# Attention scores by pairs of heads: f16 parts on two 64-row tiles, q turned by DMA, scales per token and for all keys

## The chip, the core and the metric

The kernel runs on one core of a Trainium2 chip. The metric is the device time of one execution in microseconds; the median of three runs of the kernel before is 1756.97 us (1756.92 to 1758.68). The profile shown is of one further execution, which took 1763.98 us; its span is 1762.1 us.

The engines are PE (matmul; PEld are its weight loads), DVE (vector), ACT (activation functions, copies with a scale), POOL (a slower vector engine) and SP, whose queue issues DMA transfers. Each engine runs its own instructions in order, and waits on semaphores for those of others.

## The reference

Two layers over 256 tokens of width 2048, with a context of 256 tokens. Layer 0 is a Fourier branch, layer 1 attention with 64 query heads of width 64 and 8 key heads; then a final norm. The part that the change touches, cut:

```python
q = _axial_rope(q.reshape(b, n, ATTN_Q_HEADS, ATTN_HEAD_DIM), rows, cols)
k = _axial_rope(k.reshape(b, n, ATTN_KV_HEADS, ATTN_HEAD_DIM), rows, cols)
...
s = jnp.einsum('bqhgd,bkhd->bhgqk', q, k).astype(jnp.float32) * (ATTN_HEAD_DIM ** -0.5)
s = jnp.where(mask, s, NEG_INF)
p = jax.nn.softmax(jnp.concatenate([s, sk], axis=-1), axis=-1)[..., :-1]
return jnp.einsum('bhgqk,bkhd->bqhgd', p.astype(v.dtype), v)
...
y = jnp.moveaxis(o, 0, 1).reshape(b, n, D_BRANCH) * jax.nn.silu(z)
x = x + gate * (y @ w_out[i])
```

The keys of a query are those of a window and the context, 512 columns in all; `sk` is a learned sink per head. All inputs are float32.

## The kernel before, in words

float32 products are made of parts. An operand is split into a high part (rounded) and a low part (what is left), as fp32r or as f16 with a scale, and a product is three matmuls, high by high, high by low and low by high (`mm3`, lines 145 to 147).

**Layer 1** starts at some 1085 us with the projections of keys and values, and its attention runs from 1132 to some 1610 us. The projections of q and of the gate z, and the first column block of the output product, are cut into *units* (`emit_unit`): 12 matmuls of 512 columns for q, 24 of 256 for z. A unit needs a wh and a wl, the parts of its weights: SP loads 1 MB of raw weights for two units (`raw`, line 50), ACT makes wh (line 66), DVE makes wl (line 67). Two of these tiles per unit and six buffers let the split run at most three units ahead. Units are put between the steps of attention, so that PE has work while the softmax runs on the other engines.

**Attention** is done for the 64 heads one after another. A *group* is the eight heads of one key head, a *block* a pair of heads (b = 0 to 31).

- When the eight units of a group's q are done, `finish_q` copies q out of PSUM (line 1357) and applies the rotary embedding, on POOL except for group 0. `prep_kk` makes the key parts kkh (ACT) and kkl (POOL, line 1346), both halves of the 128 partitions alike.
- `q_turn` turns q on PE with fp32 transposes (line 1370, eight a group), ACT copies the high part (lines 1373, 1374), and DVE subtracts it to get the low part (lines 1375, 1376). High and low part of one head lie above each other in the 128 partitions, so that one matmul with kkh gives two of the three products.
- `stage_s` is S(i), for one head: per 128 tokens two matmuls of fp32r (lines 1483, 1484), a mask and a minimum on DVE (line 1485, the *mask reduction*), then on ACT the exponential p (1488) and the sink's es (1489), on DVE the sum sm and its reciprocal (1490, 1491), then f, the f16 parts of the normalised p (ACT 1500, DVE 1501). A DMA transpose on SP's queue (line 1503) turns each f to ft.
- `stage_o` is P·V, O(b), for a pair of heads: 24 matmuls of 64 output columns (line 1519). The two heads use the two halves of the array's columns, so they come as couples.
- For the last three heads, PE turns f instead (`stage_t`, line 1510).

**The order.** The program is written as: S(i), a unit, after every second head O of the pair before, a unit. A scheduler takes that as a priority and fixes each engine's order ahead of time; on the chip it does not change. PSUM has eight banks of 512 columns. Tiles p and f have three buffers, ft four.

Of the kernel before, what the change touches and what calls it, by code (L numbers as in the profile page):

```python
# [32 lines left out]
def tile_dit(ctx: ExitStack, tc: tile.TileContext, a: dict, out: bass.AP):  # L33
# [10 lines left out]
    def psum():  # L44
        return pp.tile([P, 512], F32, tag="ps", name="ps")
# [1094 lines left out]
    with tc.tile_pool(name="h1", reuse_waits="tile", bufs=16) as h1p:  # L1140
        hx1 = []
        v01, vs = [], []
        dsc = h1p.tile([P, 8], F32, name="dsc", bufs=1)
        kT = []
        with tc.tile_pool(name="kvp", reuse_waits="tile", bufs=2) as kvp:
            hz, ends = [], []
# [75 lines left out]
            for tb in range(4):  # L1222
                t, ab = act(), act(F32R)
                S.copy(t, o[tb][1])
                S.activation(ab, o[tb][1], AF.Abs)
                vs.append((t, ab))
                t = act()
                if tb < 2:
                    roped(t, o[tb][0], tb, actp, "act", tab=ropek)
                else:  # L1230
                    S.activation(t, o[tb][0], AF.Copy, scale=dnk)
                kr.append(t)

            sums2(True)
            V.tensor_reduce(yq[:, 17:18], scn, axis=AX.X, op=ALU.add)
            l1 = psum()
            for tb in range(4):
                PE.matmul(l1, oner, vs[tb][1], start=tb == 0, stop=tb == 3)
            l1s, up_, ex = act(), act(), act(I32)
            V.tensor_scalar(l1s, l1, 2.0**-96, None, op0=ALU.max)  # L1240
            V.tensor_scalar(ex, l1s.bitcast(I32), 23, None, op0=ALU.logical_shift_right)
# [18 lines left out]
        with tc.tile_pool(name="at", reuse_waits="tile", bufs=2) as at:  # L1260
# [61 lines left out]
            ident16 = []  # L1322

            def k_turn(hp):
                o = psum()
                for tb in range(4):
                    PE.transpose(o[:, tb * P : (tb + 1) * P], kr[tb][:, hp * P : (hp + 1) * P], ident)
                t = act()
                S.copy(t, o)
                kT.append(t)  # L1330

            def d_turn(half):
# [3 lines left out]
                V.tensor_scalar(dsc[:, half * 4 : half * 4 + 4], o[:, 0::P], dnk, None, op0=ALU.mult)  # L1336

            def prep_kk(hk):
                kkh = at.tile([P, 512], F32R, tag="kkh", name="kkh")
                kkl = at.tile([P, 512], F32R, tag="kkl", name="kkl")  # L1340
                b = (hk % 2) * 64
                src = kT[hk // 2][b : b + 64, :]
                for c in (0, 64):
                    S.copy(kkh[c : c + 64, :], src)
                for c in (0, 64):
                    GP.tensor_tensor(kkl[c : c + 64, :], src, kkh[b : b + 64, :].bitcast(F32), op=ALU.subtract)
                kk[hk] = (kkh, kkl)

            def finish_q(hk, oq):
                qr = []  # L1350
                for tb in range(2):
                    t = act()
                    if hk == 0:
                        roped(t, oq[tb], tb, actp, "act")
                    else:
                        t0 = act()
                        S.copy(t0, oq[tb])
                        roped(t, t0, tb, actp, "act", GP)
                    qr.append(t)
                if hk:  # L1360
                    prep_kk(hk)
                for p2 in range(2):
                    defer.append((slot[0], lambda p2=p2: q_turn(hk, p2, qr)))

            def q_turn(hk, p2, qr):
                o = psum()
                for pr in range(2):
                    for tb in range(2):
                        c = (p2 * 2 + pr) * P
                        PE.transpose(o[:, (pr * 2 + tb) * P : (pr * 2 + tb + 1) * P], qr[tb][:, c : c + P], ident)  # L1370
                qa = at.tile([P, 512], F32R, tag="qa", name="qa", bufs=3)
                qb = at.tile([P, 512], F32R, tag="qb", name="qb", bufs=3)
                S.copy(qa[0:64, :], o[0:64, :])
                S.copy(qb[64:128, :], o[64:128, :])
                V.tensor_tensor(qa[64:128, :], o[0:64, :], qa[0:64, :].bitcast(F32), op=ALU.subtract)
                V.tensor_tensor(qb[0:64, :], o[64:128, :], qb[64:128, :].bitcast(F32), op=ALU.subtract)
                qq[hk, p2] = (qa, qb)

            def units():
                order = [("q", 0)]  # L1380
# [86 lines left out]
                if blk % 2:  # L1467
                    ypairs.append(slot[0] // 2)

            def stage_s(i):  # L1470
                hk, blk, hh = i // 8, i // 2, i % 2
                p2, pr = (blk % 4) // 2, blk % 2
                kkh, kkl = kk[hk]
                q2 = qq[hk, p2][hh]
                pt = [at.tile([P, 512], F32, tag="p", name="p", bufs=3) for _ in range(2)]
                mx = at.tile([P, 2], F32, tag="mx", name="mx")
                sm = at.tile([P, 2], F32, tag="sm", name="sm")
                es = at.tile([P, 2], F32, tag="es", name="es")
                so = []
                for tb in range(2):  # L1480
                    o = psum()
                    st = q2[:, (pr * 2 + tb) * P : (pr * 2 + tb + 1) * P]
                    PE.matmul(o, st, kkh, start=True, stop=False)  # L1483
                    PE.matmul(o, st, kkl, start=False, stop=True)  # L1484
                    V.tensor_tensor_reduce(o, o, mask[:, tb, :], -0.125, nsink[:, i : i + 1], ALU.add, ALU.min, mx[:, tb : tb + 1])
                    so.append(o)
                for tb in range(2):
                    S.activation(pt[tb], so[tb], AF.Exp, bias=mx[:, tb : tb + 1], scale=-1.0, accum_out=sm[:, tb : tb + 1])
                S.activation(es, mx, AF.Exp, bias=sink[:, i : i + 1])
                V.scalar_tensor_tensor(sm, sm, 1.0 / PS, es, op0=ALU.mult, op1=ALU.add)  # L1490
                V.reciprocal(sm, sm)
                ft = at.tile([P, 8, 2, P], F16, tag="ft", name="ft", bufs=4)
                fs = []
                for tb in range(2):
                    if i < 61:
                        f = at.tile([P, 1024], F16, tag="f", name="f", bufs=3)
                    else:
                        f = actp.tile([P, 1024], F16, tag="act", name="f")
                        fs.append(f)
                    fa = S.activation(f[:, 0:512], pt[tb], AF.Copy, scale=sm[:, tb : tb + 1]).ins  # L1500
                    f_last[:] = fa, V.scalar_tensor_tensor(f[:, 512:1024], pt[tb], sm[:, tb : tb + 1], f[:, 0:512], op0=ALU.mult, op1=ALU.subtract).ins  # L1501
                    if i < 61:
                        nc.sync.dma_start_transpose(ft[:, :, tb, :], f)
                return ft, fs

            def stage_t(ft, fs):
                for tb in range(2):
                    o = pp.tile([P, 8, P], F16, tag="ps", name="ps")
                    for j in range(8):
                        PE.transpose(o[:, j, :], fs[tb][:, j * P : (j + 1) * P], ident16[0])  # L1510
                    (S.copy if tb == 0 else V.tensor_copy)(ft[:, :, tb, :], o)

            def stage_o(i, pair):
                hk, blk = i // 8, i // 2
                oo = psum()[:, 0:N]
                steps = [(kb, c, j) for kb in range(4) for c, j in ((0, kb), (64, kb), (0, 4 + kb))]
                for n, (kb, c, j) in enumerate(steps):
                    for hh, ft in enumerate(pair):
                        PE.matmul(oo[hh * 64 : hh * 64 + 64, :], v01[kb][:, hk, c : c + 64], ft[:, j, :, :].rearrange("p t q -> p (t q)"), start=n == 0, stop=n == len(steps) - 1)  # L1519
                obs[blk, 1] = oo  # L1520
                emit_y(blk)

            first = 10
            for i in range(first):
# [7 lines left out]
                if i >= 8 and defer:  # L1532
                    defer.pop(0)[1]()

            def filler():
                j = slot[0]
# [3 lines left out]
                    defer.pop(0)[1]()  # L1540

            pts = {}
            for i in range(66):
                if i % 8 == 0:
                    while defer:
                        defer.pop(0)[1]()
                if i == 61:
                    t = actp.tile([P, 1024], F16, tag="act", name="ident16")
                    ident16.append(t[:, 0:P])
                    S.copy(ident16[0], ident)  # L1550
                y_sums(12, i if i < 60 else 99)
                if i == 62:
# [255 lines left out]
```

## Time and profile before

| what | number |
|---|---|
| median of three runs | 1756.97 us |
| the profiled execution, and its span | 1763.98 us, 1762.1 us |
| PE busy up to 1084 us (layer 0 and what leads to layer 1) | 1062.96 of 1084 us |
| PE busy from 1084 to 1132 us (keys, values, first q) | 48.00 of 48 us |
| PE busy from 1132 to 1590 us (attention) | 456.00 of 458 us |
| DVE, ACT, POOL busy in the same 458 us | 407.87, 358.52, 123.69 us |
| mean busy share of the DMA engines there | 0.85 |
| PE busy from 1590 to 1762 us (end) | 163.34 of 172 us |

Matmuls are pipelined, so the length that a row gives for one is longer than the step from one start to the next; costs on PE are read from starts. The "granted clock" is the share of its full clock that PE got. In a row of a group of instructions stand the line, the engine, the operation, output<-inputs and shapes, the count, then busy time and mean length in ns, then the engine's idle time ahead of them with what ended it. A row of the chain of waits has its start, its length and what it is; "DMA ft<-f" there is a wait for a transpose.

### The profile page before, as it was taken

To read this page: it belongs to the slowest core of one execution; us is meant where nothing else is said; L and a number is where in the kernel's file an instruction comes from. 1 tells how busy PE (TensorE), PEld (TensorE's weight loads), DVE (VectorE), ACT (ScalarE), POOL (GpSimd) and SP (SyncE) were. 2 spreads that over 40 slices of the span, in tenths; PEclk is the share of its full clock that TensorE was granted. 3 is DMA by queue.
4 is the path that set the end of the run, shared out by engine and by line. 5 is a ranking of instruction groups with operands and counts; after the bars stand their busy time and mean duration, and the time that the engine had idled before them with its cause. 6 is when DMAs were issued, how large, how long until landed. Compare 5 with 4: busy or idle time off the path is not lost.

```text
span 1762.1 us, 28142 instructions
## 1 busy us (share of the span) xinstructions
PE 1730.3 (98%) x10307; PEld 1174.1 (67%) x10307; DVE 1395.5 (79%) x2379; ACT 1118.5 (63%) x2101; POOL 360.9 (20%) x485
## 2 busy tenths in 40 slices
PE   6999999999999999999999999999999999999998
PEld 4679999644444444446444745888889888987464
DVE  5779889797776787777689585988899889987755
ACT  5545556477777755465235496777778777787643
POOL 0002111211222105212310210322303221251001
PEclk9999999999999999999999899999999999999999
DMA  9998999778998969977987595489997889878643
GB/s 394 417 355 251 279 273 259 286 285 310 334 314 301 315 225 381 367 258 259 396 314 228 174 350 195 165 197 220 217 207 206 215 213 215 211 191 278 225 171 120
DMA packets 232299, 465.74 MB, mean 264 GB/s; under 512 B 154496, under 2 KB 154896, under 8 KB 205280
## 3 DMA queue, kind: packets, MB, share of 16 engines
q1 hardware_dynamic: 180672, 331.41, 57.8%
q0 software_dynamic: 47344, 125.58, 22.4%
q10 hardware_dynamic: 4144, 6.95, 1.2%
q8 instruction: 81, 1.33, 0.3%
q14 instruction: 58, 0.48, 0.1%
HBM read 419.30 MB, written 12.59 MB: 245 GB/s over the span
## 4 chain that ended last, share of the span: by engine, by line
PE 76%; DVE 3%; ACT 1%; DMA 1%; issue 1%; POOL 0%; POOLq 0%; ACTq 0%; DVEq 0%
PE ps L145 23%; PE ps L146 23%; PE ps L147 23%; PE ps L1519 3%; PE ps L1484 2%; PE ps L1483 2%; ACT act L877 0%; DMA ft<-f 0%; ACT wf L137 0%; DVE wl L67 0%; DVE wf L138 0%; DVE act L878 0%; DMA sink<-in_sink 0%; PE ps L1370 0%; PE ps L997 0%
## 5 line engine op out<-in xcount | busy, mean ns | idle before, releaser
L67 DVE TENSOR_TENSOR wl<-raw,wh 128x1024 fp32r<-128x1024 f32 x152 | 211.5, 1393 | 54.9 <-ACT wh L66 44.9
L66 ACT CAST wh<-raw 128x1024 fp32r<-128x1024 f32 x152 | 158.9, 1046 | 90.2 <-PE ps L146 73.0
L146 PE MATMUL ps<-act,wf 128*128 128x512 f16 x512 | 194.0, 379 | 0.0
L147 PE MATMUL ps<-act,wf 128*128 128x512 f16 x512 | 191.1, 379 | 0.0
L145 PE MATMUL ps<-act,wf 128*128 128x512 f16 x512 | 189.8, 379 | 0.6 <-ACT wf L137 0.3
L145 PE MATMUL ps<-y,wf 128*128 128x512 f16 x448 | 169.8, 379 | 0.8 <-ACT wf L137 0.8
L146 PE MATMUL ps<-y,wf 128*128 128x512 f16 x448 | 169.8, 379 | 0.0
L145 PEld LDWEIGHTS <-wf 128*128 128x128 f16 x960 | 93.7, 98 | 113.4 <-ACT wf L137 4.2
L147 PEld LDWEIGHTS <-wf 128*128 128x128 f16 x960 | 93.9, 98 | 113.1
L146 PEld LDWEIGHTS <-wf 128*128 128x128 f16 x960 | 93.9, 98 | 109.0
L147 PE MATMUL ps<-y,wf 128*128 128x512 f16 x448 | 164.9, 379 | 0.0
L137 ACT ACTIVATE wf<-raw,nrm 128x1024 f16<-128x1024 f32 x56 | 63.4, 1145 | 133.6 <-PE ps L147 73.7
L145 PE MATMUL ps<-h,wh 128*128 128x256 f32 x512 | 145.2, 284 | 0.0
L147 PE MATMUL ps<-h,wl 128*128 128x256 f32 x512 | 143.4, 280 | 0.0
L146 PE MATMUL ps<-h,wh 128*128 128x256 f32 x512 | 143.3, 280 | 0.0
L138 DVE SCALAR_TENSOR_TENSOR wf<-raw,tn,wf 128x1024 f16<-128x1024 f32 x64 | 79.8, 1282 | 42.5 <-ACT wf L137 42.4
L829 ACT ACTIVATE act<-act 128x512 f32<-128x512 f32 x178 | 109.4, 616 | 5.4 <-DMA act<-in_wo 5.1
L1500 ACT ACTIVATE f<-p,sm 128x512 f16<-128x512 f32 x128 | 88.3, 717 | 36.2 <-DMA ft<-f 26.5
L790 POOL DMA_DIRECT2D wa<-in_adw x64 | 34.0, 532 | 375.1 <-PE ps L147 142.3
L1501 DVE SCALAR_TENSOR_TENSOR f<-p,sm,f 128x512 f16<-128x512 f32 x128 | 101.5, 823 | 7.6 <-ACT f L1500 7.2
L146 PE MATMUL ps<-wl,h 128*128 128x512 f32 x256 | 101.4, 396 | 0.0
L147 PE MATMUL ps<-wh,h 128*128 128x512 f32 x256 | 101.1, 396 | 0.0
(426 smaller groups left out, 4895.9 us busy)
## 6 DMA issues: line engine op xcount, KB each, us to landing
raw<-in_wz SPq DMA_DIRECT2D x64, 1024.0 KB, 5.7
raw<-in_awp SPq DMA_DIRECT2D x32, 1024.0 KB, 12.8
zr<-in_adw SPq DMA_DIRECT2D x64, 512.0 KB, 7.1
wa<-in_adw POOLq DMA_DIRECT2D x64, 512.0 KB, 6.7
act<-in_wo POOLq DMA_DIRECT2D x128, 256.0 KB, 7.3
raw<-in_wo SPq DMA_DIRECT2D x32, 1024.0 KB, 8.5
raw<-in_wq SPq DMA_DIRECT2D x32, 1024.0 KB, 5.5
raw<-in_wu SPq DMA_DIRECT2D x32, 1016.0 KB, 6.9
```

Source lines behind the costliest of these rows:

```text
L66: last_cast[0] = S.copy(h, src).ins
L67: last_sub[0] = eng.tensor_tensor(l, src, h.bitcast(F32), op=ALU.subtract).ins
L137: last_cast[0] = S.activation(w[:, 0], src, AF.Copy, scale=up).ins
L138: last_sub[0] = V.scalar_tensor_tensor(w[:, 1], src, up, w[:, 0], op0=ALU.mult, op1=ALU.subtract).ins
L145: PE.matmul(o, wh, xh, start=start, stop=False)
L146: PE.matmul(o, wh, xl, start=False, stop=False)
L147: return PE.matmul(o, wl, xh, start=False, stop=stop).ins
L829: S.activation(t, t, AF.Square, accum_out=c)
L1483: PE.matmul(o, st, kkh, start=True, stop=False)
L1500: fa = S.activation(f[:, 0:512], pt[tb], AF.Copy, scale=sm[:, tb : tb + 1]).ins
L1501: f_last[:] = fa, V.scalar_tensor_tensor(f[:, 512:1024], pt[tb], sm[:, tb : tb + 1], f[:, 0:512], op0=ALU.mult, op1=ALU.subtract).ins
L1519: PE.matmul(oo[hh * 64 : hh * 64 + 64, :], v01[kb][:, hk, c : c + 64], ft[:, j, :, :].rearrange("p t q -> p (t q)"), start=n == 0, stop=n ...
```

## The change

Scores are made for a pair of heads at once, from f16 parts. The new `q_parts` scales q per token by a power of two (from a sum of squares, ACT lines 1365 and 1370 of the changed kernel and four short DVE operations) and splits it to f16. The turned tile qt has one head of a pair in partitions 0 to 63 and the other in 64 to 127. For groups 1 to 7 two DMA transposes on SP's queue turn it (line 1390), for group 0 PE does with 16 f16 transposes (line 1397). Per 128 tokens a pair takes six f16 matmuls (line 1504): three products, each once on the upper 64 rows of the array and once on the lower 64, to two PSUM banks. The keys get one scale for all (four sums of squares on ACT, four short matmuls, three short DVE operations), and the mask reduction takes a scale per token in place of -0.125. In `stage_s(b)` the four mask reductions, four exponentials, two es, one sm, one reciprocal (of 128x4), four f's and four transposes of a pair follow each other. P·V of the pair before comes two units after S(b), then two more units. Tiles p and f have four buffers. Only the last pair is turned on PE at the end, 32 transposes where there were 48.

```diff
 def finish_q(hk, oq):
+    sq = at.tile([P, 2, 4], F32, tag="sq", name="sq")
...
                     t0 = act()
                     S.copy(t0, oq[tb])
+                    S.activation(act(), oq[tb], AF.Square, accum_out=sq[:, tb, 0:1])
                     roped(t, t0, tb, actp, "act", GP)
...
-    for p2 in range(2):
-        defer.append((slot[0], lambda p2=p2: q_turn(hk, p2, qr)))
-def q_turn(hk, p2, qr):
-    o = psum()
-    for pr in range(2):
-        for tb in range(2):
-            c = (p2 * 2 + pr) * P
-            PE.transpose(o[:, (pr * 2 + tb) * P : (pr * 2 + tb + 1) * P], qr[tb][:, c : c + P], ident)
-    ...
+    for tb in range(2):
+        defer.append((slot[0], lambda tb=tb: q_parts(hk, tb, qt, qr[tb], up[:, tb : tb + 1])))
+def q_parts(hk, tb, qt, qr, up):
+    f = actp.tile([P, 1024], F16, tag="act", name="fq")
+    S.activation(f[:, 0:512], qr, AF.Copy, scale=up)
+    V.scalar_tensor_tensor(f[:, 512:1024], qr, up, f[:, 0:512], op0=ALU.mult, op1=ALU.subtract)
+    if hk:
+        nc.sync.dma_start_transpose(qt[:, :, tb, :], f)
+    else:
+        pe_turn(qt, f, tb)
-def stage_s(i):
+def stage_s(b):
...
     for tb in range(2):
-        o = psum()
-        st = q2[:, (pr * 2 + tb) * P : (pr * 2 + tb + 1) * P]
-        PE.matmul(o, st, kkh, start=True, stop=False)
-        PE.matmul(o, st, kkl, start=False, stop=True)
-        V.tensor_tensor_reduce(o, o, mask[:, tb, :], -0.125, ...
+        for hh in range(2):
+            so[hh, tb] = psum()
+        for n, (jj, kx_) in enumerate(((j, kkh), (4 + j, kkh), (j, kkl))):
+            for hh in range(2):
+                r = slice(hh * 64, hh * 64 + 64)
+                PE.matmul(so[hh, tb], qt[r, jj, tb, :], kx_[r, :], start=n == 0, stop=n == 2)
+        for hh in range(2):
+            V.tensor_tensor_reduce(o, o, mask[:, tb, :], sc[:, tb : tb + 1], ...
...
 pts = {}
-for i in range(66):
+for b in range(33):
...
-    if i < 64:
-        pts[i] = stage_s(i)
-    if i - 2 >= 61:
-        stage_t(*pts[i - 2])
+    if b < 32:
+        pts[b] = stage_s(b)
     filler()
-    if i >= 2 and i % 2:
-        stage_o(i - 2, [pts.pop(j)[0] for j in (i - 3, i - 2)])
+    filler()
+    if b:
+        ft, fs = pts.pop(b - 1)
+        for (hh, tb), f in fs.items():
+            pe_turn(ft[hh], f, tb)
+        stage_o(b - 1, ft)
+    filler()
     filler()
```

How the instruction orders change, at three places. First PE at the start of attention: the first P·V matmul, and what stands around it. Before, it stands between two units of z (output<-h,wh is a matmul of z, output<-wh,h one of q), behind 31 matmuls of q and 24 of z that come after the first scores:

```order
L145 MATMUL ps<-h_10424,wh 128x256
L146 MATMUL ps<-h_10424,wh 128x256
L147 MATMUL ps<-h_10424,wl 128x256
L1519 LDWEIGHTS v
L1519 MATMUL ps<-ft,v 64x256
L145 MATMUL ps<-h_10429,wh 128x256
L146 MATMUL ps<-h_10429,wh 128x256
```

Of the changed kernel, the same place:

```order
L1504 MATMUL ps<-kkh,qt 128x512
L1504 LDWEIGHTS qt
L1504 MATMUL ps<-kkl,qt 128x512
L1538 LDWEIGHTS v
L1538 MATMUL ps<-ft,v 64x256
L145 MATMUL ps<-h_10256,wh 128x256
L146 MATMUL ps<-h_10256,wh 128x256
```

It now stands right behind S(1), whose second half (six matmuls, L1504) follows the last unit of q of group 1. Ahead of that unit are S(0) and the first half of S(1), and nothing else since S(0). The z unit (`h_10256` on) is behind it.

Second, SP's queue in the steady part: what turns the f's (ft<-f), with the weight loads (raw) between. Before:

```order
L50 DMA raw<-in_wq 128x2048
L1503 DMA_TRANSPOSE ft<-f 128x8x128 x2
L50 DMA raw<-in_wq 128x2048
L1503 DMA_TRANSPOSE ft<-f 128x8x128 x2
L50 DMA raw<-in_wz 128x2048
```

and the changed kernel, from the first transposes of attention on:

```order
L50 DMA raw<-in_wz 128x2048 x4
L1529 DMA_TRANSPOSE ft<-f 128x8x128 x8
L50 DMA raw<-in_wq 128x2048
L1390 DMA_TRANSPOSE qt<-fq 128x8x128 x2
L50 DMA raw<-in_wq 128x2048
L1529 DMA_TRANSPOSE ft<-f 128x8x128 x4
L50 DMA raw<-in_wq 128x2048 x2
L1529 DMA_TRANSPOSE ft<-f 128x8x128 x4
```

The transposes of a pair have moved together, blocks 0 and 1 have no load between their eight, and q's two stand between two loads.

Third, DVE at the start of attention, in the changed kernel (L1507 is the mask reduction, its second row the read of the minimum; `sq` are the scales of the next q):

```order
L1507 ISA ps,mx<-ps,mask,nsink,sq 128x512
L1507 ISA mx 128x1
L67 TENSOR_TENSOR wl<-raw,wh 128x1024
L1376 TENSOR_SCALAR sq<-sq 128x2
L1527 SCALAR_TENSOR_TENSOR f<-p,sm,f 128x512
L1377 TENSOR_SCALAR sq<-sq 128x2
L1527 SCALAR_TENSOR_TENSOR f<-p,sm,f 128x512
L1378 TENSOR_SCALAR sq<-sq 128x2
L1379 TENSOR_SCALAR sq<-sq,ksc 128x2
L1527 SCALAR_TENSOR_TENSOR f<-p,sm,f 128x512 x2
```

These rows follow six mask reductions and the first pair's sm and reciprocal; the first of them is the eighth. The four f's of block 0 have moved behind all eight reductions, where before the first two f's followed the sixth, and the scales of q stand between them.

More of the change, by code (lines that the diff above doesn't have):

```diff
@@ L1238, in tile_dit @@
                 PE.matmul(l1, oner, vs[tb][1], start=tb == 0, stop=tb == 3)
+            ks = psum()[:, 0:1]
+            for tb in range(4):
+                PE.matmul(ks, ones.broadcast_to([P, P]), ksc[:, tb : tb + 1], start=tb == 0, stop=tb == 3)
+            V.tensor_scalar(kx, ks, 2.0**-70, None, op0=ALU.max)
+            V.tensor_scalar(kx.bitcast(I32), kx.bitcast(I32), 24, 23, op0=ALU.logical_shift_right, op1=ALU.logical_shift_left)
+            V.tensor_scalar(ku.bitcast(I32), kx.bitcast(I32), -1.0, 204.0 * 2**23, op0=ALU.mult, op1=ALU.add)
             l1s, up_, ex = act(), act(), act(I32)
@@ L1328, in k_turn @@
                 t = act()
-                S.copy(t, o)
+                S.activation(t, o, AF.Copy, scale=ku)
                 kT.append(t)
@@ L1379, in units, with pe_turn @@
+            def pe_turn(ft, f, tb):
+                o = pp.tile([P, 8, P], F16, tag="ps", name="ps")
+                for j in range(8):
+                    PE.transpose(o[:, j, :], f[:, j * P : (j + 1) * P], ident16)
+                (S.copy if tb == 0 else V.tensor_copy)(ft[:, :, tb, :], o)
             def units():
@@ new lines, in stage_s @@
+                qt, sc = qq[hk]
+                pt = {}
+                mx, sm, es = (at.tile([P, 2, 2], F32, tag=n_, name=n_) for n_ in ("mx", "sm", "es"))
+                so = {}
+                for tb in range(2):
+                    for hh in range(2):
[5 more added lines that the diff above has]
+                    for hh in range(2):
+                        o = so[hh, tb]
+                        V.tensor_tensor_reduce(o, o, mask[:, tb, :], sc[:, tb : tb + 1], nsink[:, 2 * b + hh : 2 * b + hh + 1], ALU.add, ALU.min, mx[:, hh, tb : tb + 1])
@@ L1491, in stage_s @@
                 V.reciprocal(sm, sm)
-                ft = at.tile([P, 8, 2, P], F16, tag="ft", name="ft", bufs=4)
-                fs = []
+                ft = [at.tile([P, 8, 2, P], F16, tag="ft", name="ft", bufs=4) for _ in range(2)]
+                fs = {}
                 for tb in range(2):
[L1495 to L1503, printed above, removed]
@@ L1504, in stage_s @@
-                return ft, fs
[L1506 to L1514, printed above, removed]
+                    for hh in range(2):
+                        if b < 31:
+                            f = at.tile([P, 1024], F16, tag="f", name="f", bufs=4)
+                        else:
+                            f = actp.tile([P, 1024], F16, tag="act", name="f")
+                            fs[hh, tb] = f
+                        s1 = sm[:, hh, tb : tb + 1]
+                        fa = S.activation(f[:, 0:512], pt[hh, tb], AF.Copy, scale=s1).ins
+                        f_last[:] = fa, V.scalar_tensor_tensor(f[:, 512:1024], pt[hh, tb], s1, f[:, 0:512], op0=ALU.mult, op1=ALU.subtract).ins
+                        if b < 31:
+                            nc.sync.dma_start_transpose(ft[hh][:, :, tb, :], f)
@@ L1531, in tile_dit @@
                         d_turn(half)
-                if i >= 8 and defer:
-                    defer.pop(0)[1]()
+            while defer:
+                defer.pop(0)[1]()
             def filler():
```

57 lines of the change are left out of this document (27 added, 30 removed).

## The prediction

> **What bounds the kernel now.** I read the page first: how full PE is, and what the chain of work that ended last is made of.
>
> ```profile
> span 1762.1 us, 28142 instructions
> PE 1730.3 (98%) x10307; PEld 1174.1 (67%) x10307; DVE 1395.5 (79%) x2379; ACT 1118.5 (63%) x2101; POOL 360.9 (20%) x485
> PE 76%; DVE 3%; ACT 1%; DMA 1%; issue 1%; POOL 0%; POOLq 0%; ACTq 0%; DVEq 0%
> ```
>
> PE is busy for 98% of the span, and 76% of the chain is PE. Next I cut the attention stage into windows, because an average over the whole program says nothing of it. In a row: the window and its length, busy time (and count) of PE, PEld, DVE, ACT and POOL, then granted clock, DMA share, GB/s.
>
> ```profile
> 1164.00:1168.00 4.00, 2.50 (x18) 2.11 (x16) 3.85 (x6) 2.46 (x4) 0.00 (x0) 1.00 1.19 200
> 1168.00:1172.00 4.00, 3.50 (x28) 2.89 (x29) 3.76 (x10) 2.38 (x7) 0.00 (x0) 0.60 1.20 289
> 1229.00:1288.00 59.00, 59.00 (x420) 51.61 (x419) 53.98 (x93) 45.93 (x88) 14.79 (x10) 1.00 0.92 218
> ```
>
> The third row is one group of four blocks (eight heads) in the steady part: PE has no gap, DVE is busy for 53.98 of 59 us (91%), and the DMA engines for 0.92. So each microsecond of PE's work taken out there is worth a microsecond, as long as DVE and the DMA queue, which are nearly full, keep up. The first two rows show the stage's one real stall: PE has 2.50 of 4 us, and the clock granted after it is 0.60.
>
> **What leaves PE.** The chain of waits gives the period of a block by the starts of its P·V bursts (line 1519):
>
> ```profile
> 1226.75 1.43 PE ps L1519 x24
> ...
> 1270.81 1.43 PE ps L1519 x24
> ...
> 1286.45 1.43 PE ps L1519 x24
> ```
>
> From the first to the second row are three blocks, 14.69 us each; the block up to the third row has the eight q transposes of a group (line 1370) in it and takes 15.64. They therefore cost 0.95 us. Groups 1 to 7 lose them: 7 x 0.95 = **6.7 us saved**. Group 0 has 16 f16 transposes for 8 of fp32; by the rows of line 1510 below that is 0.9 for 0.9, nothing.
>
> The scores of a pair, from the timeline (start, length; the pipelined length isn't the pitch, the starts are):
>
> ```profile
> 1084.18 0.38 PE L147 MATMUL ps<-wf,hz 128*128 128x512 f16 x1
> ...
> 1086.12 0.38 PE L147 MATMUL ps<-wf,hz 128*128 128x512 f16 x1
> ...
> 1231.05 0.39 PE L1483 MATMUL ps<-kkh,qa 128*128 128x512 f32 x1
> ...
> 1231.73 0.40 PE L1484 MATMUL ps<-kkl,qa 128*128 128x512 f32 x1
> ```
>
> and, from the chain again, the matmuls right behind two P·V bursts and a usual one:
>
> ```profile
> 1228.18 0.31 PE ps L145
> ...
> 1238.89 0.23 PE ps L146
> ...
> 1242.88 0.43 PE ps L145
> ```
>
> In the timeline's last two rows three steps take 0.68 us, 0.227 each, or 0.91 for a head's four; a pair's eight take 1.84 (the other head steps a little wider). An f16 matmul of 512 columns steps by (1086.12 - 1084.18) / 9 = 0.216. The change has 12 of these per pair, in six couples on two tiles of 64 rows. Before has no such form. The nearest row is the P·V burst, whose 24 matmuls run as couples on two 64-column tiles: 12 couples of 256 columns, at half of 0.216 each 1.29 us with full overlap, take 1.43, and the next matmul takes 0.31 or 0.43 where 0.23 is usual, so going in and out costs about 0.14 + 0.13. I give the row tiles the same: 6 x 0.216 + 0.27 = 1.56, so 0.28 per pair, 32 x 0.28 = **9.0 us saved**. Bounds: nothing for the switch (1.30 per pair, 17 us saved), and no overlap at all (12 x 0.216 + 0.27 = 2.86, a loss of 32.6; a rival below).
>
> The Trainium skill, "TensorEngine Tiling (Array Packing)", section Key Properties, says that tiles work in parallel and that a change of tiling mode drains TensorE. The P·V burst agrees with both (1.43 us for 24 matmuls, 0.27 around them); nothing in before's trace shows it for row tiles.
>
> Small ones. At the end block 31 alone is turned on PE, so 32 f16 transposes replace 48:
>
> ```profile
> 1612.04 1.07 PE L1510 MATMUL ps<-ident,f 128*128 128x128 f16 x16
> L1290 PE MATMUL ps<-adab,ones 128*128 128x1 f32 x6 | 0.8, 222 | 0.0
> ```
>
> Sixteen take 1.07 with the last one's pipeline, some 0.9 in a full stream: **0.9 saved** (0 if the tail there waits for something else). The keys' scale adds four fp32 matmuls of one column, at most 0.222 each when nothing overlaps; I take **0.4 lost** (0 to 0.9). Sum so far 6.7 + 9.0 + 0.9 - 0.4 = 16.2 us.
>
> **What is moved: the first block.** Scores of two heads now come at once, and PE runs the P·V of block 0 after the scores of block 1. By the instruction order PE has after S(0) only S(1) and one unit of twelve matmuls, then the first P·V matmul; a z unit is queued behind it. Before, these rows:
>
> ```profile
> 1132.20 0.40 PE L1483 MATMUL ps<-kkh,qa 128*128 128x512 f32 x1
> ...
> 1146.01 0.30 PE L1519 MATMUL ps<-ft,v 128*64 128x256 f16 x1
> ```
>
> and on DVE, ACT and SP's queue:
>
> ```profile
> 1133.34 0.76 DVE L1485 CUSTOM_DVE_ANT_0 ps<-ps,mask,nsink 128x512 f32<-128x512 f32 x1
> ...
> 1134.02 0.75 DVE L1485 CUSTOM_DVE_ANT_0 ps<-ps,mask,nsink 128x512 f32<-128x512 f32 x1
> ...
> 1137.72 1.22 DVE L67 TENSOR_TENSOR wl<-raw,wh 128x1024 fp32r<-128x1024 f32 x1
> ...
> 1145.39 2.93 DVE L1501 SCALAR_TENSOR_TENSOR f<-p,sm,f 128x512 f16<-128x512 f32 x2
> ...
> 1139.33 1.05 ACT L66 CAST wh<-raw 128x1024 fp32r<-128x1024 f32 x1 [0.29 <-PE ps L146]
> ...
> 1141.66 0.59 ACT L1357 COPY act<-ps 128x512 f32<-128x512 f32 x1
> ...
> 1143.10 1.33 ACT L1500 ACTIVATE f<-p,sm 128x512 f16<-128x512 f32 x2
> ...
> 1175.23 0.63 ACT L1284 ACTIVATE act<-act 128x512 f32<-128x512 f32 x1
> 1175.76 0.19 ACT L1284 ACTIVATION_READ_ACCUMULATOR act<-act 128x1 f32 x1
> ...
> 1139.68 2.71 SPq L1503 DMA_TRANSPOSE ft<-f  x2
> ```
>
> There PE had 13.8 us of other work between the first score and the first P·V matmul. After it has about 1.56 (S(0)), 12 x 0.233 = 2.8 (the unit) and 1.56 (S(1), cut in two): it stands at the P·V 5.9 us after S(0)'s start. When is its operand there? On ACT, in order: four exps, over by then; once that unit ends, at 5.1, a copy and a square of q, a weight cast, another copy and square (2 x 0.59 + 2 x 0.82 + 1.05, to about 9.0); then the f's at 0.67. On DVE eight mask reductions at 0.67, a wl (1.22), then four f's; from the first copy POOL is at the rope, and with it running two f's took 2.93. So f number 3, the second that the first P·V matmul needs, is ready at 9.6 + 3 x 1.47 = 14.0 (at 0.74 each, as without POOL, 11.8). The transposes follow on SP's queue:
>
> ```profile
> L1503 SPq DMA_TRANSPOSE ft<-f x122: 1231/1286/4614, 1139.7 to 1590.1; - x122
> DMA to landing us min/median/max: 3.1/5.7/8.1
> 1160.37 8.08 DMA ft<-f
> 1168.50 2.54 PE ps L1519 x23
> ```
>
> At 3.5 us, near the least (the queue has no weight load among these eight), it lands at 17.5: PE is idle for 17.5 - 5.9 = 11.6 us. Bounds: 11.8 + 3.1 gives 9.0; with the median 5.7 it is 13.8. Afterwards comes a slow clock: the last two rows are before's stall, where PE waited for a transpose (2.0 us idle, see the first two windows) and the P·V of 23 matmuls then took 2.54 for 1.43, 1.1 us more. For the longer gap I charge the 0.40 not granted in the 4 us of that second window, 1.6. The old stall should go, since the f's of block 1 stand right behind those of block 0 and a z unit and S(2) lie ahead of its P·V: -2.0 - 1.1. Net 11.6 + 1.6 - 3.1 = **10.1 us lost** (7 to 14 by these bounds).
>
> The Trainium skill, "TensorE: Matmul & The Clock Gate", Part 1, says that after an idle window of some 3.4 us the clock is halved until some 3.4 us of work; an estimate from that page would be 1.7 us for the 1.6, so the sum is the same. The 0.60 granted after a gap of only 2.0 us shows that less idle time is enough here.
>
> **The steady blocks.** DVE and ACT trade work:
>
> ```profile
> L1375 DVE TENSOR_TENSOR qa<-ps,qa 64x512 fp32r<-64x512 f32 x16 | 10.9, 684 | 0.5
> L1501 DVE SCALAR_TENSOR_TENSOR f<-p,sm,f 128x512 f16<-128x512 f32 x128 | 101.5, 823 | 7.6 <-ACT f L1500 7.2
> L67 DVE TENSOR_TENSOR wl<-raw,wh 128x1024 fp32r<-128x1024 f32 x138 | 194.4, 1410 | 35.1 <-ACT wh L66 34.3 <-PE ps L1519 0.5
> L1490 DVE SCALAR_TENSOR_TENSOR sm<-sm,es 128x2 f32<-128x2 f32 x64 | 17.2, 269 | 1.3 <-ACT es L1489 1.0
> L1488 ACT ACTIVATE p<-ps,mx 128x512 f32<-128x512 f32 x128 | 87.6, 686 | 17.9 <-DVE mx L1485 14.6 <-DVE f L1501 2.1
> L1373 ACT CAST qa<-ps 64x512 fp32r<-64x512 f32 x16 | 9.1, 569 | 0.0
> ```
>
> Per group DVE loses four subtractions (4 x 0.69 = 2.8) and gains two fq (2 x 0.82) and four tiny ones (some 0.6): 0.6 less. ACT loses four copies (2.3) and gains two squares (2 x 0.82) and two fq (2 x 0.7): 0.7 more of some 57 us. Both are hidden under PE while a block has 14.4 us. SP's queue gets two q transposes more per group, and the four f transposes of a block in one run, where before had two and two with a load between. The fourth lands, from S(b)'s start: scores 0.9, reductions 2.7, exp 0.7 and the short es, sm and reciprocal 0.8, two wl 2.8, first f 0.8, three more issues at 1.29 = 3.9, landing 5.7 (the median), in all 18.3. P·V of b comes one block, S(b+1) and two units (2.8 each) later: 14.4 + 1.56 + 5.6 = 21.5. Slack 3 us. Where a group's q is finished, copies, squares and fq stand ahead and POOL runs: perhaps 3 us late, so 0 to 1 us of stall each; I take 0.33 x 6 = **2 us lost** (0 to 13).
>
> **Sum.** -16.2 + 10.1 + 2 = -4.1 against the profiled execution, whose own time was 1763.98 us for the span of 1762.1; that run is 7.0 above the median of the runs shown, 1756.97. The same difference on the median gives **1752.9 us**, 0.23% faster. A measurement here tells a difference from none at about 0.2%, 3.5 us, so this sits at the border.
>
> **Rivals.**
> 1. The first block does not stall so: the f's come earlier, or PE's queue still holds work. Then some 2 us are left of the 10.1: -16.2 + 2 + 2 = -12.2, 1745. For it: DVE is idle for 9% of the stage. Against: what is queued behind the P·V matmul can't pass it. Chance 0.17.
> 2. The run of four transposes is late in every block; this is the slower side. Place: PE at the P·V, waiting for the fourth transpose. It decides once the 18.3 passes 21.5: with the landing at 8.1, the maximum above, and one more wl (1.4) ahead, it is 22.1, and each block loses up to 0.6. At 0.4, 32 x 0.4 = 13 in place of the 2: -4.1 + 11 = +6.9, 1764. For it: DMA share 0.92, DVE 91%, ACT's f's already wait for transposes. Against: only one such wait of PE in before. Chance 0.2.
> 3. The row tiles overlap badly. Each matmul of a couple writes all 128 partitions of a bank, where the column tiles wrote 64 each, so a couple may step by anything from 0.216 to 0.431. It breaks even with before at (1.84 - 0.27) / 6 = 0.262. At 0.28 a pair takes 1.95, 32 x 0.11 = 3.5 lost in place of 9.0 saved: -4.1 + 12.5 = +8.4, 1765. One after the other, 2.86 a pair, 32.6 lost, while the longer block takes the 2 away: 1793. The column tiles speak against both. Chance 0.15, mostly the first.
> 4. The change does what it says, at about my sizes: 1747 to 1759. Chance 0.48.
>
> On the third, the Trainium skill, "TensorE: Matmul & The Clock Gate", Part 3, gives 3.07 times for four row tiles, 0.77 of full; an estimate from that page is 0.28 a couple. No run here shows it yet.
>
> Of the fourth, 0.25 lies below 1753.5, 0.17 around no change, 0.06 above; with the first (all faster), the second (0.05 no change, 0.15 slower) and the third (0.03 and 0.12) this gives 0.42 faster, 0.25 the same, 0.33 slower. Range 1741 to 1772: at the low end the first rival with nothing lost at either place (-16.2); at the high end the second at 0.6 a block, 1770, with some of the first gap's upper bound. It leaves out the worse half of the third. The fourth's own range is 1747 to 1759.
>
> **What would show it.** The chain after the change should have intervals of 14.4 us between P·V bursts, the same in all four blocks of a group; line 1504's couples should start together, every 0.216 us. PE should have one gap of 9 to 14 us just after the first scores, ended by the transpose, and granted clock near 0.5 behind it, and the stretch at 1164 full. I am wrong if couples start 0.216 apart one by one, if the windows of the steady part show PE below 58 of 59 us, or if the first gap is missing.

## The result, and the profile after

The changed kernel takes 1780.01 us (median of 4 runs, 1778.66 to 1782.05) against 1757.24 us before; the ratio is 1.0129, with a 95% interval of 1.0111 to 1.0146. It is 22.8 us slower; 1752.9 was forecast, with a range up to 1772. The profiled execution took 1778.66 us.

The head of its page, and two windows that answer to those of before (columns as there):

```profile
span 1776.9 us, 28302 instructions
PE 1717.7 (97%) x10379; PEld 1134.2 (64%) x10379; DVE 1385.8 (78%) x2334; ACT 1112.8 (63%) x2125; POOL 342.2 (19%) x485
```

```profile
1132.00:1170.00 38.00, 23.38 (x182) 18.64 (x183) 27.58 (x49) 24.30 (x51) 9.55 (x8) 0.82 0.50 113
...
1229.00:1288.00 59.00, 56.55 (x416) 45.94 (x417) 50.21 (x81) 44.05 (x88) 11.66 (x10) 1.00 0.84 216
```

PE is busy for less time in all (1717.7 us against 1730.3), so work was taken out as intended; but it now waits. At the start of attention it is busy for 23.38 of 38 us at a clock of 0.82, and in the steady part, where before had no gap in 59 us, 2.45 us are missing. DVE is less busy there than before (50.21 for 53.98 us), so no engine has become full.

Who made PE wait, from the view of waits (total, times, longest), first of the changed kernel, then the one such row of before:

```profile
PE ps L1538 <- ACT f L1526: 14.6, 1, 14.6
...
PE ps L1538 <- DMA ft<-f: 7.1, 12, 1.0
PE ps L147 <- DVE wl L67: 6.2, 7, 1.0
PE ps L146 <- DVE wl L67: 2.8, 1, 2.8
```

```profile
PE ps L1519 <- DMA ft<-f: 2.0, 1, 2.0
```

30.7 us for 2.0. The first row is the gap at the first P·V, for which 11.6 us were forecast. It names f on ACT, but block 0's f's were done there at 1144.2; what the P·V at 1152.88 needed last was block 0's third transpose, issued at 1149.55 and landed 3.2 us later. The granted clock was 0.50 in the 4 us from 1152 on. The second and third rows lie at the ends of the groups (13.3 us; forecast 2); the fourth, near the end of attention, was not forecast.

The chain of waits at the end of one group, with the blocks before it:

```profile
1482.20 1.40 PE ps L1504 x12
1483.60 0.32 PE ps L145
...
1504.11 1.43 PE ps L1538 x24
...
1518.53 1.43 PE ps L1538 x24
...
1525.86 4.41 DVE f L1527 x4
1530.27 1.45 DVE wl L67 x2
1531.72 4.13 DMA ft<-f
1535.89 1.50 PE ps L1538 x23
```

The scores of a pair take 1.40 us for twelve matmuls, so the row tiles run at the same time; the block between the two P·V bursts takes 14.42 us, as forecast. The next takes 17.36, up to the second matmul of its P·V (in four of the six groups it is 15.8 to the first). There the chain leaves PE, and goes through the four f's on DVE (4.41 us for four) and the last transpose to the P·V. The 1.45 us between them are put down to wl, but SP is issuing the third transpose then (at 1530.34, for 1.29 us).

A word on the base. The first profiled execution of before (1763.98 us) was slower than any of 20 other runs of that kernel (1755.79 to 1760.42). Between the spans of the two profiles the loss is only 14.8 us, between the medians 22.8.

### The profile page after: what moved, and what is told of

Same layout as the page of the kernel before. It is cut to its first block, busy times and chain, and to the rows that moved or that the text cites. A ratio compares the mean times of both kernels' runs of the same rounds, so it can differ in the third digit from the quotient of the medians.

```text
span 1776.9 us, 28302 instructions
## 1 busy us (share of the span) xinstructions
PE 1717.7 (97%) x10379; PEld 1134.2 (64%) x10379; DVE 1385.8 (78%) x2334; ACT 1112.8 (63%) x2125; POOL 342.2 (19%) x485
## 3 DMA queue, kind: packets, MB, share of 16 engines
q1 hardware_dynamic: 197568, 335.60, 57.9%
## 5 line engine op out<-in xcount | busy, mean ns | idle before, releaser
L67 DVE TENSOR_TENSOR wl<-raw,wh 128x1024 fp32r<-128x1024 f32 x152 | 191.5, 1270 | 101.8 <-ACT wh L66 85.8
L1511 ACT ACTIVATE p<-ps,mx 128x512 f32<-128x512 f32 x128 | 87.8, 687 | 89.1 <-DVE mx L1507 84.9
L145 PEld LDWEIGHTS ps<-h,wh 128*128 128x128 f32 x512 | 96.8, 189 | 10.0 <-ACT th L1474 4.2
```

The source lines that it names most:

```text
L67: last_sub[0] = eng.tensor_tensor(l, src, h.bitcast(F32), op=ALU.subtract).ins
L145: PE.matmul(o, wh, xh, start=start, stop=False)
L1511: S.activation(pt[hh, tb], so[hh, tb], AF.Exp, bias=mx[:, hh, tb : tb + 1], scale=-1.0, accum_out=sm[:, hh, tb : tb + 1])
```

## The experiments

**Before once more.**

> The kernel before, profiled once more, because its first profiled execution (1763.98 us) lay 7 us above the median of its runs while that of the changed kernel (1778.66 us) lies at its own. Theory: the 7 us lie outside attention (before 1132 us of the span), so the change's true cost is 14.7 us within attention and the rest is another chip: then this run has its first scores near 1125 us and the attention as before. Rival: the 7 us lie within attention, and the first profile showed a stall that the usual run does not have (the 2.0 us gap near 1166 us and the slow clock behind it are candidates): then first scores at 1132 us and attention shorter by 7.

It took 1760.54 us, with a span of 1758.8. Its first scores began at 1130.33 us (1132.20 in the first profile) and its last P·V at 1617.24 (1620.64). So of the 3.4 us between the two profiles 1.9 lie ahead of the first scores; the other 1.5 lie between these and the fifth P·V, and from there on the two take the same time. Neither account in the expectation is right by itself. The view of waits has the same row as the first profile, 2.0 us: the stall is the usual one. The slow clock behind it is not: here the granted clock in the 4 us behind it is 1.00, not 0.60, and the P·V of 23 matmuls takes 1.50 us, not 2.54.

**The scales behind the f's.** In the changed kernel the four short DVE operations on q's scales stand among or ahead of the f's of the block in which a group's q is finished. The rows on DVE in the first block, and at the end of a group:

```profile
1142.25 0.69 DVE L1376 TENSOR_SCALAR sq<-sq 128x2 f32<-128x2 f32 x1
1142.85 1.83 DVE L1527 SCALAR_TENSOR_TENSOR f<-p,sm,f 128x512 f16<-128x512 f32 x1
1144.61 0.69 DVE L1377 TENSOR_SCALAR sq<-sq 128x2 int32<-128x2 int32 x1
1145.21 1.29 DVE L1527 SCALAR_TENSOR_TENSOR f<-p,sm,f 128x512 f16<-128x512 f32 x1
1146.43 1.22 DVE L1378 TENSOR_SCALAR sq<-sq 128x2 int32<-128x2 int32 x1
1147.56 1.31 DVE L1379 TENSOR_SCALAR sq<-sq,ksc 128x2 int32<-128x2 int32 x1
1148.78 1.40 DVE L1527 SCALAR_TENSOR_TENSOR f<-p,sm,f 128x512 f16<-128x512 f32 x2
...
1277.80 0.70 DVE L1376 TENSOR_SCALAR sq<-sq 128x2 f32<-128x2 f32 x1
1278.54 1.22 DVE L1377 TENSOR_SCALAR sq<-sq 128x2 int32<-128x2 int32 x1
1279.79 0.67 DVE L1378 TENSOR_SCALAR sq<-sq 128x2 int32<-128x2 int32 x1
1280.37 0.79 DVE L1379 TENSOR_SCALAR sq<-sq,ksc 128x2 int32<-128x2 int32 x1
1281.07 4.87 DVE L1527 SCALAR_TENSOR_TENSOR f<-p,sm,f 128x512 f16<-128x512 f32 x4
```

and on POOL, beside the second of these stretches:

```profile
1278.43 1.30 POOL L1132 TENSOR_TENSOR act<-act,rope 128x512 f32<-128x512 f32 x1
1279.69 1.44 POOL L1137 TENSOR_TENSOR rt<-act,rope 128x256 f32<-128x256 f32 x2
1281.08 2.98 POOL L1138 TENSOR_TENSOR act<-act,rt 128x512 f32<-128x512 f32 x2
```

Four operations on two columns take 3.9 and 3.4 us, and the four f's behind them 4.87 where POOL still runs. DVE does not stand idle between them: the operations themselves are longer. The edit:

```diff
-V.tensor_scalar(x, sq[:, :, 0], 2.0**-70, None, op0=ALU.max)
...
+with tc.issue_after(f_last[1]) if hk else nullcontext():
+    V.tensor_scalar(x, sq[:, :, 0], 2.0**-70, None, op0=ALU.max)
...
```

> The four short DVE operations on q's scales of groups 1 to 7 are put behind the f's of the block instead of ahead of them; nothing else is changed. Theory A (they stand ahead of the f's, wait for POOL's rotary work, take 3.4 to 3.9 us, and make the transposes and so P.V late): the gap in the first block falls from 14.6 to about 10.7 us, the P.V waits at the ends of the groups (some 2.3 us each, seven times) nearly vanish, time near 1760 us. Rival B (SP's queue with q's two transposes and the runs of four is what is late): 1777 to 1781 us, waits as before. Rival C (POOL slowing the f's themselves is enough): half of A, near 1770.

1778.53 us (ratio to before 1.0121, 1.0104 to 1.0138): next to nothing won. Its waits of PE, and its windows at the end of a group:

```profile
PE ps L1539 <- DMA ft<-f: 12.0, 2, 11.7
PE ps L145 <- ACT wh L66: 4.8, 6, 0.8
PE ps L147 <- DVE wl L67: 4.5, 6, 0.8
PE ps L146 <- DVE wl L67: 2.8, 1, 2.8
```

```profile
1412.00:1416.00 4.00, 2.44 (x16) 2.04 (x15) 2.97 (x7) 4.00 (x9) 0.00 (x0) 0.90 0.83 150
1416.00:1420.00 4.00, 4.00 (x26) 3.07 (x25) 4.00 (x6) 3.90 (x6) 0.00 (x0) 0.67 1.33 280
```

The first gap fell from 14.6 to 11.7, as theory A says, and the transposes were in time: 0.3 us is all that is left of their 7.1. But the same blocks now wait for wh and wl, 0.8 us each, and the clock is 0.67 in the 4 us behind (a slow clock follows these waits in the last four of the six groups; behind the same two waits of the first group it is 1.00, from 1234 to 1238). So A holds for the first block and for who was late at the P·V, but its 1760 is missed by 18 us: at the ends of the groups the delay is still there, at other operations. The time is the one that rival B named, the waits are not.

**q turned on PE.**

```diff
-if hk:
-    nc.sync.dma_start_transpose(qt[:, :, tb, :], f)
-else:
-    pe_turn(qt, f, tb)
+pe_turn(qt, f, tb)
```

> All groups' q are turned on PE with 16 f16 transposes, as group 0 already is, so no DMA transposes of q on SP's queue. Theory A: the waits at the ends of the groups stay, since the f's are as late as before; PE gets 7 x 0.9 = 6 us more; near 1786 us. Rival B (q's transposes in SP's queue make the others late): the waits vanish (16 us), less 6 for PE: near 1770.

1793.22 us (ratio 1.0207, 1.0192 to 1.0223). Without q's transposes in SP's queue nothing is won. The wl waits stay (6.0 us), and PE, now with q's transposes in its order, waits for fq on ACT (7.0 us) and DVE (4.2 us). The waits of P·V for the transposes are gone, but with PE held up ahead of them this run alone does not decide against rival B. What does is late_scales above and no_rope below: both leave SP's queue as it was, and at the ends of the groups all but 0.3 us of these waits are gone.

**More work ahead of the first P·V.**

```diff
 filler()
 filler()
+if b == 1:
+    filler()
+    filler()
 if b:
     ...
     stage_o(b - 1, ft)
-filler()
-filler()
+if b != 1:
+    filler()
+    filler()
```

> In the second step of the loop all four units are written ahead of the first P.V instead of two ahead and two behind; all else as in the changed kernel. Theory D (PE's order: the gap is long because too little work stands ahead of the first P.V): two units of z, 5.6 us, fill the gap of 14.6, which falls to about 9; time near 1774. Rival: the gap only moves, since the z units wait for their own weights behind the same DVE queue: no change, 1780.

1776.38 us (ratio 1.0106, 1.0091 to 1.0121). The gap fell from 14.62 to 8.90 us, the length of two units, and 3.6 us of it reached the end: theory D holds.

**Without POOL's rotary work.**

```diff
-roped(t, t0, tb, actp, "act", GP)
+t = t0
```

> The rotary work on q of groups 1 to 7 (POOL, seven instructions of about 9 us in all per group) is left out; q goes unrotated to the scores of those groups. Scales, squares and all orders as in the changed kernel. Theory A2 (POOL's rotary work slows DVE just in the blocks where the scales stand ahead of the f's: four short operations 3.4 us instead of 0.6, four f's 4.9 us instead of 2.9): the P.V and wl waits at the ends of the groups vanish, 13 to 16 us, and the first gap shrinks from 14.6 to about 9; time near 1757 to 1760. Rival E (the squares and copies of q on ACT, ahead of the f's, are enough to be late): at most a third of that, near 1774.

1758.13 us (ratio 1.0003, 0.9993 to 1.0012): 21.9 us less than the changed kernel. The groups of instructions on DVE between 1200 and 1500 us, first of the changed kernel, then of this one:

```profile
L1527 DVE SCALAR_TENSOR_TENSOR f<-p,sm,f 128x512 f16<-128x512 f32 x80 | 65.8, 878 | 0.0
L1507 DVE CUSTOM_DVE_ANT_0 ps<-ps,mask,nsink 128x512 f32<-128x512 f32 x77 | 58.8, 815 | 0.0
...
L1377 DVE TENSOR_SCALAR sq<-sq 128x2 int32<-128x2 int32 x5 | 6.1, 1222 | 0.2
```

```profile
L1507 DVE CUSTOM_DVE_ANT_0 ps<-ps,mask,nsink 128x512 f32<-128x512 f32 x84 | 64.1, 816 | 0.0
L1527 DVE SCALAR_TENSOR_TENSOR f<-p,sm,f 128x512 f16<-128x512 f32 x83 | 57.1, 746 | 0.0
...
L1377 DVE TENSOR_SCALAR sq<-sq 128x2 int32<-128x2 int32 x5 | 0.8, 170 | 0.2
```

Without POOL the short operation takes 170 ns for 1222 and an f 746 for 878, while the mean of the mask reduction, which reads and writes scores in PSUM, is 815 or 816 either way. All waits at the ends of the groups are gone, and the first gap is 11.2 us. Squares and copies on ACT were as before, and so were the orders on PE, DVE, ACT and SP; so rival E falls.

**The same work, put elsewhere.** Here nothing is left out. The rotary work on POOL starts when its input is copied from PSUM on ACT; that copy, and the square, now stand behind the block's f's, and scales and fq behind those of the next block.

```diff
-t0 = act()
-S.copy(t0, oq[tb])
-S.activation(act(), oq[tb], AF.Square, accum_out=sq[:, tb, 0:1])
+with tc.issue_after(f_last[0]):
+    t0 = act()
+    S.copy(t0, oq[tb])
+    S.activation(act(), t0, AF.Square, accum_out=sq[:, tb, 0:1])
...
+def parts(tb):
+    with tc.issue_after(f_last[0]) if hk else nullcontext(), tc.issue_after(f_last[1]) if hk else nullcontext():
+        if hk and not tb:
+            q_scales(x, up, sc, sq)
+        q_parts(hk, tb, qt, qr[tb], up[:, tb : tb + 1])
```

> Nothing is left out. Copies and squares of a finished q are put behind the block's f's on ACT, so that POOL's rotary work starts when these f's are nearly done; the scales and the split of q behind the f's of the next block. Theory A2: DVE meets POOL on other operations that have slack, the waits at the ends of the groups vanish (16 us) and the first gap falls to about 8 us: near 1757 to 1762. Rival F (wherever POOL's work falls, DVE has no slack for it in a block of 14.4 us): the waits move to wl and wh, as they did in late_scales, near 1778.

1757.71 us (ratio to before 1.0001, 0.9992 to 1.0011): 22.3 us less than the changed kernel, with all its work kept: the order is moved, and the square reads the copy in place of PSUM. POOL and DVE at the end of a group:

```profile
1272.09 2.86 POOL L1137 TENSOR_TENSOR rt<-act,rope 128x256 f32<-128x256 f32 x2
...
1278.54 2.55 POOL L1138 TENSOR_TENSOR act<-act,rt 128x512 f32<-128x512 f32 x2
```

```profile
1275.04 2.24 DVE L67 TENSOR_TENSOR wl<-raw,wh 128x1024 fp32r<-128x1024 f32 x1 [0.68 <-ACT wh L66]
1277.20 0.81 DVE L1518 CUSTOM_DVE_ANT_0 ps<-ps,mask,nsink 128x512 f32<-128x512 f32 x1
...
1288.31 0.16 DVE L1391 TENSOR_SCALAR sq<-sq 128x2 f32<-128x2 f32 x1
```

POOL still slows a wl (2.24 us for 1.22), but the rest of its run lies beside the mask reductions, which it doesn't slow (0.81 us), and a short operation, now behind POOL's run, takes 0.16 us again. P·V has no wait in the six groups between but one of 0.55 us; 10.55 are left in the first gap. Rival F falls.

**Both edits.**

> As q_late, and the two units of z ahead of the first P.V as in o0_late. Theory: the two edits act on different places and add up: q_late less 5 us (two units, 5.6 us, fill most of the gap that is left), near 1753, below the kernel before. Rival: with the first gap filled DVE runs behind with wl, and only half of it is won.

1751.65 us (ratio 0.9968, 0.9955 to 0.9981), 0.3% faster than before. The first gap is 4.76 us. The order of P·V on PE was then moved once more:

```diff
 filler()
+if b == 2:
+    stage_o(0, pts.pop(0)[0])
 filler()
...
-if b:
+if b > 1:
     ft, fs = pts.pop(b - 1)
```

> As q_late_o0, and the first P.V comes one unit later still, behind S(2) and 38 more matmuls of z (1.4 + 4.5 us against the 4.8 that were left of the gap). Theory: the gap closes and the time falls by 4 to 5 us more, to about 1747. Rival: block 2 starts before block 0's transposed tiles are free, its own transposes wait, and the gap comes back at the second or third P.V: 1751 as in q_late_o0.

1751.60 us (ratio 0.9966, 0.9954 to 0.9977), the same as q_late_o0. The gap at the first P·V is closed, and 3.30 us of waiting for a transpose came up at the second: the rival, as to the outcome. Whether the tiles ft were the reason was not tried.

**The order on the two row tiles.**

```diff
-for n, (jj, kx_) in enumerate(((j, kkh), (4 + j, kkh), (j, kkl))):
-    for hh in range(2):
+for hh in range(2):
+    for n, (jj, kx_) in enumerate(((j, kkh), (4 + j, kkh), (j, kkl))):
```

> The six matmuls of 128 tokens are ordered by head, three on the upper 64 rows, then three on the lower, instead of alternating. If the two tiles run at the same time only for neighbours in the order, a pair's scores take about 12 x 0.216 + 0.2 = 2.8 us instead of 1.4, and the time rises by up to 32 x 1.4 = 45 us (less what the waits at the ends of the groups hide, some 15), near 1810. If order doesn't matter: 1.4 us and 1780.

1769.58 us in a single run. The second account has the 1.4 us right, but not the time. PE's timeline in one pair's scores:

```profile
1312.63 0.61 PE L1504 MATMUL ps<-kkh,qt 64*128 64x512 f16 x4
1313.07 0.39 PE L1504 MATMUL ps<-kkl,qt 64*128 64x512 f16 x2
1313.29 0.60 PE L1504 MATMUL ps<-kkh,qt 64*128 64x512 f16 x4
1313.72 0.39 PE L1504 MATMUL ps<-kkl,qt 64*128 64x512 f16 x2
1314.03 0.50 PE L145 MATMUL ps<-wh,h 128*128 128x512 f32 x1
```

1.40 us from the first start to the next unit, as in the changed kernel, with the four kkh matmuls started ahead of both kkl though the program has one head's kkl third. The time is 10.4 us less though the scores take as long: with this edit the scheduler also moved DVE's and ACT's order, and the waits for wl (6.2 and 2.8 us) are not there. Which of these moves did it was not tried.

## Why the prediction was wrong

Point by point, by its own steps:

- **What bounds the kernel**: right, PE's gaps are what the time is made of. That a microsecond out of PE is worth one "as long as DVE and the DMA queue keep up" named the condition, and it failed. The prediction's own sign of being wrong came true: PE is busy for 56.55 of 59 us in the steady part, below 58.
- **Scores, 9.0 us saved**, and **q's transposes, 6.7**: right in mechanism, a little high. 1.40 us for the twelve, and 14.42 us for a plain block (14.4 forecast). In q_late_o0, where nothing hides it, four blocks run as follows:

```profile
1218.39 1.43 PE ps L1549 x24
...
1276.30 1.43 PE ps L1549 x24
```

  57.91 us for the 59.70 of before (1226.75 to 1286.45): 1.79 a group for the 2.07 (4 x 0.28 + 0.95) of the sum. The third rival falls, and with it the 0.28 a couple estimated beside it.
- **The first block, 11.6 us of gap**: right in place and kind, 3.0 us too small. The step that failed is "On DVE eight mask reductions at 0.67, a wl (1.22), then four f's": the four scale operations stand among these f's in the order, and were left out of this chain. They took 3.9 us. With them behind, late_scales has the gap at 11.7. The old stall is gone, as forecast, but of its -2.0 and -1.1 the slow clock's 1.1 was not to be had on the median: before_again has the stall without it.
- **The steady blocks, "0.33 x 6 = 2 us lost"**: this is the step that turned the sign. The waits there are 13.3 us. On PE's timeline of the changed kernel the fifth and the twenty-ninth P·V stand at

```profile
1212.80 1.50 PE L1538 MATMUL ps<-ft,v 128*64 128x256 f16 x24
...
1579.82 1.50 PE L1538 MATMUL ps<-ft,v 128*64 128x256 f16 x24
```

  so that six groups take 367.0 us, 61.2 each, where q_late_o0 takes 57.9: 3.3 a group, not 0.33. Before takes 358.4 for these 24 blocks (1210.99 to 1569.40), with as much work of q and z in them (12 matmuls of 512 columns more, 24 of 256 fewer); with the sum's savings (24 x 0.28 and 6 x 0.95) and its 2 us of loss it would be 348.0. So 19.0 us of the miss lie here.

  The term that was mis-sized is "perhaps 3 us late", with "Slack 3 us" against it. In the group whose chain is shown above, the last f ends 18.95 us after the start of its scores, and in the plain block ahead of it 13.07: 5.9 us late. Two prices made it. "Four tiny ones (some 0.6)" took 3.4, since each was lengthened beside POOL, and they stand ahead of the f's. The f's themselves took 4.87 for four, where the row of the whole stage had 823 ns for one, a mean over blocks with and without POOL. no_rope and q_late show the cause: take POOL's work away, or let it fall on other operations, and the 22 us are gone. The idle time, 13.3 us, is about the 13 of the upper bound; what it cost is more.
- **The end**: a wait of 2.8 us for wl was not forecast. It stands in every kernel with the changed scores but seq_tiles, and its cause was not tried. In the trace of the changed kernel POOL is at work there too (on `ys`, from 1576.9 to 1595.6), and three f's ahead of that wl take 3.48 us.
- **Rivals**: the first falls with the gap of 14.6. The second had the place (P·V, waiting for the last transpose), but not the mechanism. It had asked for a late landing in every block; the plain blocks are on time, and SP's queue was not what was late (late_scales and no_rope, with the queue unchanged). The fourth had 1747 to 1759.
- **The clock**: stalls below 1 us were priced at their length. late_scales shows two of 0.8 us followed by 0.67 of the clock in 4 us, but not each time (1.00 behind the same two in the first group). Nor is "less idle time is enough", which the prediction read from 0.60 behind 2.0 us, so each time: before_again has 1.00 there. What decides between the two was not tried.

In waits alone the sum was short by 30.7 - 13.6 = 17.1 us. The whole miss is 27.1 (1780.0 for 1752.9), and part of the rest is that a wait costs more than its idle time, as 61.2 - 57.9 = 3.3 for 2.2 of waits a group shows. The remainder, a few us, is not accounted for; the slow first profile of before makes it hard to place.

Why q_late, with the groups 1.8 us shorter, only equals before can be read by stages, against before_again. From the fifth to the twenty-ninth P·V it takes 348.6 us for 358.4: 9.9 won. From the first scores to the fifth P·V it takes 76.30 for 77.25, but with 19 matmuls of 512 columns and 24 of 256 fewer (moved ahead of the first scores), some 7.2 us at 0.233 and 0.117 a step: 6.3 lost, with the first gap in it. From the twenty-ninth P·V to the end it takes 198.5 for 192.8, with twelve matmuls of 512 more (2.8 us): 2.9 lost, with the wait for wl in it. So 9.2 of the 9.9 are lost again at the two ends of attention.

On the cause there is a rule: the Trainium skill, "SBUF — State Buffer", section Who interferes with whom, says that DVE and GpSimd (POOL here) share one pair of ports as an exclusive lock, and of DVE's two-port modes that whoever issues first has the pair for the whole instruction, while the other blocks. The runs agree with the length: the operation at 1278.54, 170 ns without POOL, took 1.22 us and ended with the POOL instruction that had begun at 1278.43 and took 1.30; the mask reduction kept its 815 ns. That these DVE operations ran in such a mode no run shows.

## What to carry to other kernels

The busy share of an engine says nothing of a burst: DVE was less busy after the change than before, and still late in one block of four, because several heads' operations had been put one behind another and a second engine's work fell just there. Price every instruction that the order puts into the chain, the shortest too, in the company it will have there: a mean over the whole stage hides it. And when a chain is late, look first at whether the work beside it can be put elsewhere: here nearly the same instructions in another order were worth 22 to 28 us.

## What the runs showed of the hardware

- An operation on DVE of two columns takes 0.16 to 0.22 us alone (no_rope) and 0.66 to 1.31 us while POOL works on SBUF (the changed kernel); the mask reduction, which reads and writes scores in PSUM, takes 0.81 us beside POOL (1277.20 in q_late) as without it.
- Two row tiles of 64 rows run at the same time in both orders tried: three matmuls for one tile followed by three for the other took the same 1.40 us per pair as alternating ones, and started out of program order. The Trainium skill, "TensorE: Matmul & The Clock Gate", Part 3, says that matmuls start and end in program order; for the starts on different row tiles seq_tiles shows otherwise.
- The mask reduction takes 815 ns with a scale per token from SBUF and took 753 with a constant.
- The same idle time of PE can be followed by a slow clock or not: behind 2.0 us the granted clock of 4 us was 0.60 in one execution of before and 1.00 in another.
